# A hybrid attention and convolution layer: the norm of the second half of the sequence in steps of one engine's part, and the sums of w_down in fixed places of the convolution

## The chip, the cores and the metric

The kernel runs on one core of a Trainium2 chip. The metric is the device time of one execution in microseconds; the time before is the median of three runs. The engines are named as the profile names them: PE (matrix products) and PEld (its weight loads), DVE (vector), ACT (scalar, activations), POOL, and SP, which issues nearly all DMAs. Each engine works through its own instructions in order; semaphores tie the engines together.

## What is computed

The reference is one layer on a sequence of 2048 rows of width 1024, in float32:

```python
h = rmsnorm(x, norm1_g) * (1 + sc1) + sh1
proj = h @ w_in
q, k, v, fg, xin, bg, cg = jnp.split(proj, IN_SPLITS, axis=-1)
q = rmsnorm(q.reshape(b, s, ATTN_HEADS, HEAD_DIM), q_norm_g)
k = rmsnorm(k.reshape(b, s, ATTN_HEADS, HEAD_DIM), k_norm_g)
attn = forgetting_attention(q, k, v, logf).reshape(b, s, ATTN_WIDTH)
conv = bg * causal_dwconv(cg * xin, conv_mix_w)
x = x + g1 * (jnp.concatenate([attn, conv], axis=-1) @ w_out)
h2 = rmsnorm(x, norm2_g) * (1 + sc2) + sh2
u_gate, u_val = jnp.split(causal_dwconv(h2 @ w_up, ffn_conv_w), 2, axis=-1)
y = (jax.nn.silu(u_gate) * u_val) @ w_down
return x + g2 * y
```

The shifts, scales and gates (`sh1`, `sc1`, `g1`, ...) come from a small product of the condition `c`. The attention has 8 heads of 64, the convolution 512 channels with 3 taps, the feed-forward part a hidden width of 2816.

## The kernel before

**Products.** Large products run as high and low parts: an operand is split into `hi`, its rounding to a shorter format, and `lo`, what is left, and three matmuls (hi·hi, hi·lo, lo·hi) are added up. The two products of the feed-forward part also use a scheme of seven block products in place of eight, with sums and differences of blocks as operands. For `w_down`, four of these block sums per unit of 256 rows are worked out once, early in the kernel, and kept in DRAM as `w_sc`; there are 11 units (`NJ`).

**Stages.** By the trace: start, modulation and the value product to about 180 us; the k and q projections (`project`, L605 to L665) to 360; the convolution (`for j in range(4)`, L815 to L890) to 605; attention to about 935; the output product and the first residual to 1130; then, for each half of the sequence, `up` (the product with `w_up`, the 3-tap convolution and the gate) and `down` (the product with `w_down` and the last residual): `up(0)` to 1530, `down(0)` to 1777, `up(1)` to 2175, `down(1)` to 2388.

**What sets the order.** An instruction wrapped in `K` (`tc.keep_in_program_order`, L141) keeps its place among the others that are wrapped; those that are not wrapped are placed by a scheduler, in time and so on their engine. Work that runs beside the matmuls is written as Python generators, of which the main loop takes a step at fixed places. Tiles come from pools by tag; a tag with `bufs=n` has n buffers, and a new tile waits until the one before it in that buffer is done with.

**The sums of w_down.** `down_sums` (L742 to L768) loads two tiles `wd` for each unit, one unit ahead, makes four sums of 128x512 into one tile `ws` of 128x2048 (`bufs=1`), and stores it with one DMA of 1 MB. None of this is wrapped. The convolution takes one of its steps with each of its three block products (`next(wsums)`, L851), 48 in all; the first load and the three steps of each unit use 34.

**The convolution.** For each of four channel groups and four chunks of the sequence it makes the products `x`, `c` and `b` in three of six PSUM banks, 24 matmuls with three parts each; ACT and DVE then combine them (L860 to L882).

**down(0).** Its loop goes over 77 entries `e`: 7 block products `p`, each over 11 units `j`. An entry is 12 matmuls (L1643), on four accumulators; the entry of `j` = 9 is done together with `j` = 10. Each entry needs an operand pair, `raw`, read from DRAM five entries ahead and split by ACT into `hi` (L1412) and by DVE into `lo` (L1413), two entries ahead; `raw`, `hi` and `lo` have four buffers each. At `j` = 10 of a product DVE or ACT takes the four sums out of PSUM (`evict`); for p = 1, 4, 5 and 6 this makes finished blocks of the output (`finish_block`), multiplied by the gate, added to `xs` (rows of x1, read again) and stored.

**The norm of the second half.** `x1`, the sequence after the first residual, is kept in DRAM as `x1_sc`. `norm2(Q)` makes the operands of `up` for quarter `Q` of the sequence. Quarters 0 and 1 are done before `up(0)`; 2 and 3 run beside `down(0)`, as its `side` generator, which takes a step in 45 of the 77 entries (L1646). For these quarters a step loads four tiles of 128x1024 (`w<-x_sc`, L1272); then come the sums of squares on ACT (L1276), two per step, the reciprocal root on DVE, the scaling on DVE (L1283), and for each of 8 columns of 128 a transposition on PE into `pt` (L1259), the affine part on ACT (L1261), and the parts `hi` (ACT, L1242) and `lo` (DVE, L1245). For quarter 3 each k of 4 takes two columns and makes from them and the columns of quarter 2 five operands, by the sums and differences of L1252 and L1317; a step holds operations of DVE and ACT that depend on one another.

Of the kernel before, what the change touches and what calls it, by code (L numbers as in the profile page):

```python
# [20 lines left out]
P = 128  # L21
# [25 lines left out]
def kernel(  # L47
# [104 lines left out]
    with ExitStack() as ph:  # L152
# [588 lines left out]
        def down_sums():  # L741

            todo = []

            def load(j):
                ab = [lp.tile([P, D], F32, tag="wd", name="wd", bufs=4) for _ in range(2)]
                for e, w in enumerate(ab):
                    nc.sync.dma_start(w, w_down[(2 * j + e) * P : (2 * j + e + 1) * P, :])
                todo.append(ab)

            load(0)
            yield
            for j in range(NJ):
                if j + 1 < NJ:
                    load(j + 1)
                (a11, a21), (a12, a22) = [[w[:, 0:512], w[:, 512:1024]] for w in todo.pop(0)]
                t = lp.tile([P, 2 * D], F32, tag="ws", name="ws", bufs=1)
                s1, s2, s3, s4 = [t[:, n * 512 : (n + 1) * 512] for n in range(4)]
                V.tensor_tensor(s1, a21, a22, op=ALU.add)
                yield  # L760
                V.tensor_tensor(s3, a11, a21, op=ALU.subtract)
# [5 lines left out]
            while True:  # L767
                yield  # L768

        wsums = down_sums()  # L770
# [450 lines left out]
    with ExitStack() as ph:  # L1221
# [10 lines left out]
        def add_gated(acc, gate, src, dst):  # L1232

            g = temp()
            K(V.tensor_tensor(g, acc, gate, op=ALU.mult))
            K(V.tensor_tensor(src, src, g, op=ALU.add))
            nc.sync.dma_start(dst, src)

        bt = {}

        def high(raw, hi):
# [2 lines left out]
        def low(raw, hi, lo):  # L1244
            K(V.tensor_tensor(lo, raw, hi, op=ALU.subtract))  # L1245
# [18 lines left out]
        def norm2(Q):  # L1264
# [4 lines left out]
            xn[Q] = kept[Q] if Q < 2 else [wide_temp()[:, 0:D] for _ in range(4)]  # L1269
            if Q >= 2:  # L1270
                for t in range(4):
                    K(nc.sync.dma_start(xn[Q][t], x1_sc[Q * 4 + t]))  # L1272
                yield
            for t in range(4):
                junk = fp.tile([P, D], BF16, tag="t2", name="junk", bufs=NTEMP)
                K(A.activation(junk, xn[Q][t], AF.Square, accum_out=ss[:, t : t + 1]))  # L1276
# [42 lines left out]
                yield  # L1319
            if Q % 2:  # L1320
                low(t4, *t4s)
                yield

        add = lambda o, a, b: K(V.tensor_tensor(o, a, b, op=ALU.add))  # L1324
# [249 lines left out]
        def down(hv, side):  # L1574
# [13 lines left out]
            def banks(kinds):  # L1588
# [2 lines left out]
                    for k in kinds  # L1591
                ]

            def finish_block(c, n, t, total):
                g = temp()
                K(V.tensor_tensor(g, total, gate[n], op=ALU.mult))
                add(xs[c, n][t], xs[c, n][t], g)
                K(nc.sync.dma_start(out[rows[c][t], n * 512 : (n + 1) * 512], xs[c, n][t]))

            def evict(p, t):  # L1600
                a = acc[t]
                if p == 0:
                    K(A.activation(u2[t], a, AF.Copy))
                elif p == 1:
                    finish_block(0, 0, t, a)
                elif p == 2:
                    add(u2[t], u2[t], a)
                elif p == 3:
                    add(u3[t], u2[t], a)
                elif p == 5:  # L1610
                    add(u3[t], u3[t], a)
                    finish_block(1, 1, t, u3[t])
                else:
                    g = temp()
                    add(g, u2[t], a)
                    finish_block(*((0, 1) if p == 4 else (1, 0)), t, g)

            extra = {(1, 2): (0, 0), (4, 2): (0, 1), (5, 2): (1, 1), (6, 3): (1, 0)}
            for e, (p, j) in enumerate(todo):
# [15 lines left out]
                if j != NJ - 2:  # L1635
                    for t in range(4):
# [6 lines left out]
                                K(T.matmul(acc[t], lhsT=a[:, c], rhs=b, start=st, stop=sp, skip_group_check=True))  # L1643
# [45 lines left out]
```

## Time and profile before

| | |
|---|---|
| median of 3 runs | 2398.73 us (2393.88 to 2399.53) |
| the profiled execution | 2397.5 us, its span 2395.8 us |
| granted clock of PE, mean | 0.992 |
| PE, DVE, ACT busy | 95%, 73%, 48% of the span |
| `down(0)` | 1529.8 to 1776.9: 247.1 us, clock 0.96 |
| `down(1)` | 2175.5 to 2388.3: 212.8 us, clock 1.00 |

Three views are used below. The windows give for a stretch the busy time of each engine, with the count of its instructions in parentheses, and the clock that PE was granted (1.00 is full speed). The timeline gives one row for an instruction or a run of like ones: start, duration, engine, line, operation, result `<-` operands, partitions x elements, count, and in brackets how long the engine had been idle and what ended that. The waits add these idle times up by the line that waited and what it waited for. DMA rows give size and the median time from issue to landing.

### The profile page before, as it was taken

How to read it: one execution, taken by the hardware profiler on the slowest of the kernel's cores; microseconds unless marked ns; L12 is line 12 of the kernel's file. 1: busy time of each engine (PE TensorE's matmuls, PEld its weight loads, DVE VectorE, ACT ScalarE, POOL GpSimd, SP SyncE). 2: the span in 40 equal slices, each digit the busy share in tenths (PEclk: the TensorE clock that was granted, in tenths of full speed). 3: DMA queues.
4: the chain of work that ended last, by engine and by line, in shares of the span. 5: the costliest groups of instructions: out<-in, count | busy, mean ns of one | idle time of the engine just before them, and what ended most of it. 6: DMA issues, size and time to landing. Idle time of an engine off the chain costs nothing.

```text
span 2395.8 us, 38576 instructions
## 1 busy us (share of the span) xinstructions
PE 2284.4 (95%) x14208; PEld 1359.9 (57%) x14208; DVE 1738.1 (73%) x3404; ACT 1161.1 (48%) x1990; POOL 340.0 (14%) x282
## 2 busy tenths in 40 slices
PE   5899999999899898999999999999899999999998
PEld 5764444444577676444444444577764444447886
DVE  6768896653899897456999999766755555656556
ACT  5745353321688897343556556454423223224332
POOL 0211111111677784001000000000000000000000
PEclk9999999999999999999999999999999999999999
DMA  9349898632799997434565565765664544455765
GB/s 278 138 156 270 274 265 280 204 106 88 147 182 182 209 188 150 169 110 167 174 212 198 204 221 195 254 221 193 211 205 143 161 156 145 154 162 188 236 198 209
DMA packets 447895, 455.25 MB, mean 190 GB/s; under 512 B 190721, under 2 KB 300633, under 8 KB 445273
## 3 DMA queue, kind: packets, MB, share of 16 engines
q1 hardware_dynamic: 440584, 435.94, 61.7%
q10 hardware_dynamic: 4752, 8.46, 1.0%
q0 software_dynamic: 2368, 8.39, 0.9%
q8 instruction: 111, 1.82, 0.3%
q14 instruction: 80, 0.65, 0.1%
HBM read 284.84 MB, written 134.28 MB: 175 GB/s over the span
## 4 chain that ended last, share of the span: by engine, by line
PE 72%; DVE 14%; DMA 5%; ACT 4%; issue 3%; SPq 1%; POOL 0%; DVEq 0%; ACTq 0%; POOLq 0%
PE acc L1489 28%; PE acc L1643 14%; PE pr L145 10%; PE acc L145 8%; PE pv L145 2%; PE pt L1099 2%; PE ps L1038 1%; PE ps L1039 1%; DVE near L1106 1%; DMA far<-wide 1%; DVE t L1324 1%; PE po L1135 1%; DVE s_t L1062 1%; DVE lo L1413 1%; PE po L1137 1%
## 5 line engine op out<-in xcount | busy, mean ns | idle before, releaser
L1489 PEld LDWEIGHTS <-pair 128*128 128x128 f16 x3696 | 361.5, 98 | 439.7 <-issue 5.0
L1489 PE MATMUL acc<-t,pair 128*128 128x512 f16 x2112 | 477.4, 379 | 1.9 <-DVE t L1324 1.9
L1489 PE MATMUL acc<-b,pair 128*128 128x512 f16 x1584 | 363.4, 379 | 0.0
L1502 DVE SCALAR_TENSOR_TENSOR w<-w,fcw,w 128x1024 f32<-128x1024 f32 x176 | 226.1, 1285 | 79.4 <-ACT w L1497 73.4
L1413 DVE TENSOR_TENSOR lo<-raw,hi 128x1024 fp32r<-128x1024 f32 x154 | 185.2, 1223 | 128.4 <-ACT hi L1412 114.6
L1643 PE MATMUL acc<-hi 128*128 128x512 f32 x616 | 245.5, 399 | 15.0 <-ACT hi L1412 10.2
L1643 PE MATMUL acc<-lo,hi 128*128 128x512 f32 x616 | 243.9, 396 | 4.7 <-DVE lo L1413 4.7
L1643 PE MATMUL acc<-hi,lo 128*128 128x512 f32 x616 | 242.9, 394 | 0.0
L1412 ACT ACTIVATE hi<-raw 128x1024 fp32r<-128x1024 f32 x154 | 158.8, 1053 | 165.3 <-PE acc L1643 96.6
L145 PEld LDWEIGHTS <-h 128*128 128x128 f16 x1344 | 130.7, 98 | 98.7 <-DVE h L358 5.4
L1497 ACT ACTIVATE w<-w,fcw 128x1024 f32<-128x1024 f32 x88 | 100.6, 1143 | 160.9 <-DVE w L1324 160.9
L145 PE MATMUL acc<-wp,mp 128*128 128x512 f16 x768 | 171.1, 382 | 1.1 <-DVE raw L991 1.0
L1079 ACT ACTIVATE s_t<-s_t,nb,cst 128x2048 f32<-128x2048 f32 (+15 forms) x128 | 164.7, 1288 | 4.8
L1643 PEld LDWEIGHTS acc<-hi 128*128 128x128 f32 x616 | 117.5, 191 | 43.6 <-ACT hi L1412 12.3
L1091 POOL TENSOR_TENSOR wide<-s_t,wide 128x1024 f16<-128x1024 f32 x64 | 136.7, 2136 | 5.3
L1643 PEld LDWEIGHTS acc<-lo,hi 128*128 128x128 f32 x616 | 117.4, 191 | 31.4 <-DVE lo L1413 7.7
L1062 DVE CUSTOM_DVE_ANT_0 s_t<-ps,nf,mx 128x512 f32<-128x512 f32 (+1 forms) x192 | 119.5, 643 | 17.0 <-PE ps L1041 8.9
L1643 PEld LDWEIGHTS acc<-hi,lo 128*128 128x128 f32 x616 | 117.4, 191 | 24.8
L145 PE MATMUL pr<-h,wh 128*128 128x512 f16 x576 | 126.5, 379 | 0.0
L145 PE MATMUL pr<-h,wl 128*128 128x512 f16 x576 | 125.8, 379 | 0.0
L145 PEld LDWEIGHTS <-mp 128*128 128x128 f16 x768 | 75.4, 98 | 88.9 <-issue 3.4
L1038 PE MATMUL ps<-kh,qs 128*128 128x512 f16 (+1 forms) x320 | 109.6, 347 | 5.3 <-DVE mx L1062 4.4
(355 smaller groups left out, 4085.4 us busy)
## 6 DMA issues: line engine op xcount, KB each, us to landing
up_sc<-pair SPq DMA_DIRECT2D x132, 256.0 KB, 2.7
pair<-up_sc SPq DMA_DIRECT2D x132, 256.0 KB, 3.2
wx<-in_w_up_dram SPq DMA_DIRECT2D x88, 256.0 KB, 3.8
raw<-in_w_up_dram SPq DMA_DIRECT2D x44, 512.0 KB, 3.8
y_t<-t SPq DMA_DIRECT2D x88, 256.0 KB, 2.7
raw<-y_t SPq DMA_DIRECT2D x88, 256.0 KB, 4.1
raw<-w_sc SPq DMA_DIRECT2D x88, 256.0 KB, 4.2
y_b<-y SPq DMA_DIRECT2D x66, 256.0 KB, 2.1
```

The costliest lines, as they stand in the source:

```text
L145: ins = T.matmul(acc, lhsT=a, rhs=b, start=st, stop=sp)
L1038: K(T.matmul(ps[:, 0:cw], lhsT=qt, rhs=kh[:, c0 : c0 + cw], start=True, stop=False))
L1062: K(V.tensor_tensor_reduce(out=s_t[:, o0 + c0 : o0 + c0 + cw], in0=ps[:, 0:cw], in1=nf[:, c0 : c0 + cw], scale=1.0, scalar=-3.0e38 if g == ...
L1079: K(A.activation(cols, cols, AF.Exp, bias=nb[:, p : p + 1], scale=qk[:, 4:5], accum_out=un["l"][:, p : p + 1]))
L1091: K(G.tensor_tensor(wide[:, 1, :], s_t[:, WB * P : WU], wide[:, 0, :], op=ALU.subtract))
L1099: K(T.transpose(pt[:, b * P : (b + 1) * P], s_t[:, (b0 + b) * P : (b0 + b + 1) * P], ident))
L1412: K(A.activation(hi, raw, AF.Copy))
L1413: K(V.tensor_tensor(lo, raw, hi.bitcast(F32), op=ALU.subtract))
L1489: K(T.matmul(acc, lhsT=a, rhs=b, start=st, stop=sp, skip_group_check=True))
L1497: K(A.activation(y, u[:, 0:1024], AF.Copy, scale=fcw[:, ct : ct + 1]))
L1502: K(V.scalar_tensor_tensor(y, u[:, m : m + 1024], fcw[:, m * 44 + ct : m * 44 + ct + 1], y, op0=ALU.mult, op1=ALU.add))
L1643: K(T.matmul(acc[t], lhsT=a[:, c], rhs=b, start=st, stop=sp, skip_group_check=True))
```

## The change

It has two parts that don't touch each other.

The sums of `w_down`: loads, sums and stores are now wrapped in `K`, so they stand where the convolution takes a step. Each sum has a tile of its own (128x512, six buffers) and a DMA of its own (256 KB; 44 in place of 11), which is issued at the first step of the next unit.

The norm of quarters 2 and 3: `norm2_late` takes the place of `norm2`, and `down` takes a step of it in every entry. The load is issued in the first step of a quarter, two further steps do nothing, then comes one square per step. A column's transposition, its affine part with `hi`, and its `lo` stand in different steps. For quarter 3 the sums of a k (`sums`) are seven steps, of which each holds one engine's operations; they run while the next k's columns are transposed. Sixty-five entries have such work, in place of 39 steps before. `finish_block` and `evict` take their temporary `g` from the tag `first` with two buffers, no longer from `temp()` with seven.

```diff
@@ down_sums
-                    nc.sync.dma_start(w, w_down[(2 * j + e) * P : (2 * j + e + 1) * P, :])
+                    K(nc.sync.dma_start(w, w_down[(2 * j + e) * P : (2 * j + e + 1) * P, :]))
...
+            def keep(j, n, src0, src1, op):
+                t = lp.tile([P, 512], F32, tag="ws", name="ws", bufs=6)
+                K(V.tensor_tensor(t, src0, src1, op=op))
+                kept.append(lambda: K(nc.sync.dma_start(w_sc[j][:, n * 512 : (n + 1) * 512], t)))
+                return t
...
+                while kept:
+                    kept.pop(0)()
...
-                t = lp.tile([P, 2 * D], F32, tag="ws", name="ws", bufs=1)
...
-                V.tensor_tensor(s1, a21, a22, op=ALU.add)
-                yield
-                V.tensor_tensor(s3, a11, a21, op=ALU.subtract)
-                V.tensor_tensor(s2, s1, a11, op=ALU.subtract)
-                yield
-                V.tensor_tensor(s4, a12, s2, op=ALU.subtract)
-                nc.sync.dma_start(w_sc[j], t)
+                s1 = keep(j, 0, a21, a22, ALU.add)
+                yield
+                keep(j, 2, a11, a21, ALU.subtract)
+                s2 = keep(j, 1, s1, a11, ALU.subtract)
+                yield
+                keep(j, 3, a12, s2, ALU.subtract)
                 yield
@@ norm2_late (new, for Q = 2 and 3)
+            for t in range(4):
+                K(nc.sync.dma_start(xn[Q][t], x1_sc[Q * 4 + t]))
+            for _ in range(3):
+                yield
+            for t in range(4):
+                junk = fp.tile([P, D], BF16, tag="t2", name="junk", bufs=NTEMP)
+                K(A.activation(junk, xn[Q][t], AF.Square, accum_out=ss[:, t : t + 1]))
+                yield
...
+            def sums(k, b1, b2):
...
+                high(b2, b22[0])
+                diff(t3, b2, b1)
+                diff(b1, b1, b11[0])
+                diff(b1, b1, b11[1])
+                low(b2, *b22)
+                yield
+                high(b1, t1s[0])
+                high(t3, t3s[0])
+                yield
+                diff(b2, b2, b1)
+                low(b1, *t1s)
+                low(t3, *t3s)
+                yield
+                high(b2, t2s[0])
+                yield
...
+            for k in range(4):
+                first = turn(Q, k)
+                go_on()
+                yield
+                b1 = first()
+                go_on()
+                yield
+                second = turn(Q, 4 + k)
+                go_on()
+                yield
+                b2 = second()
+                go_on()
+                running.append(sums(k, b1, b2))
+                yield
@@ down
+            def rest():
+                return fp.tile([P, 1024], F32, tag="first", name="g", bufs=2)[:, 0:512]
...
-                g = temp()
+                g = rest()
...
-                if e < 3 or e % 2 == 0 or e % 7 == 1:
-                    next(side, None)
+                next(side, None)
...
-        steps = {Q: norm2(Q) for Q in range(4)}
+        steps = {Q: (norm2 if Q < 2 else norm2_late)(Q) for Q in range(4)}
```

How the rows move on the engines, at three places. First ACT in `down(0)`, where quarter 2 arrives; `hi` are the splits of `down`'s operands, `junk` the squares of the four loaded tiles. Before:

```order
L1412 ACTIVATE hi<-raw 128x1024 x5
L1276 ACTIVATE junk,ss<-w_18779 128x1024
L1276 ACTIVATE junk,ss<-w_18780 128x1024
L1412 ACTIVATE hi<-raw 128x1024 x2
L1276 ACTIVATE junk,ss<-w_18781 128x1024
L1276 ACTIVATE junk,ss<-w_18782 128x1024
L1412 ACTIVATE hi<-raw 128x1024 x2
```

And now:

```order
L1514 ACTIVATE hi<-raw 128x1024 x5
L1344 ACTIVATE junk,ss<-w_18823 128x1024
L1514 ACTIVATE hi<-raw 128x1024
L1344 ACTIVATE junk,ss<-w_18824 128x1024
L1514 ACTIVATE hi<-raw 128x1024
L1344 ACTIVATE junk,ss<-w_18825 128x1024
L1514 ACTIVATE hi<-raw 128x1024
L1344 ACTIVATE junk,ss<-w_18826 128x1024
L1514 ACTIVATE hi<-raw 128x1024
```

The squares, two and two before, now stand one by one between the splits.

Second, DVE at the end of product 4 of `down(0)`: three rows (`u,acc`, then the gate, then `xs`) are the eviction of the last of four sums, and the rows below it belong to the sums of quarter 3 (`t_...`) and to the operands of the next entries (`lo`). Before:

```order
L1324 TENSOR_TENSOR t_20051<-u,acc 128x512
L1596 TENSOR_TENSOR t_20053<-t_20051,gates 128x512
L1324 TENSOR_TENSOR xs<-xs,t_20053 128x512
L1252 TENSOR_TENSOR t_19936<-t_19936,b_19166 128x512
L1252 TENSOR_TENSOR t_19982<-t_19982,t_19936 128x512
L1245 TENSOR_TENSOR t_19987<-t_19936,t_19987 128x512
L1245 TENSOR_TENSOR t_19989<-t_19984,t_19989 128x512
L1413 TENSOR_TENSOR lo<-raw,hi 128x1024 x2
L1252 TENSOR_TENSOR t_19985<-b_19246,t_19982 128x512
```

And now:

```order
L1426 TENSOR_TENSOR g<-u,acc 128x512
L1701 TENSOR_TENSOR g<-g,gates 128x512
L1426 TENSOR_TENSOR xs<-xs,g 128x512
L1246 TENSOR_TENSOR t_19944<-t_20049,t_19944 128x512
L1253 TENSOR_TENSOR t_20022<-t_20022,t_19970 128x512
L1246 TENSOR_TENSOR t_20054<-t_19970,t_20054 128x512
L1246 TENSOR_TENSOR t_20056<-t_20058,t_20056 128x512
L1515 TENSOR_TENSOR lo<-raw,hi 128x1024 x2
L1253 TENSOR_TENSOR t_20185<-b_19350,t_20022 128x512
```

Four operations of the sums, three `lo` and one difference, stand between the eviction and `lo`; before there were two differences and two `lo`.

ACT at the same place, where `pt` is the transposed column and L1242 (now L1243) makes the `hi` of the sums. Before:

```order
L1261 ACTIVATE t_19982<-pt,sh_225,a_224 128x512
L1242 ACTIVATE b_19986<-t_19982 128x512
L1412 ACTIVATE hi<-raw 128x1024 x2
L1242 ACTIVATE t_19987<-t_19936 128x512
L1242 ACTIVATE t_19989<-t_19984 128x512
L1242 ACTIVATE t_19988<-t_19982 128x512
L1412 ACTIVATE hi<-raw 128x1024 x2
```

And now:

```order
L1243 ACTIVATE b_20053<-t_20022 128x512
L1514 ACTIVATE hi<-raw 128x1024
L1329 ACTIVATE t_20071<-pt,sh_225,a_224 128x512
L1243 ACTIVATE t_19944<-t_20049 128x512
L1243 ACTIVATE t_20054<-t_19970 128x512
L1243 ACTIVATE t_20056<-t_20058 128x512
L1514 ACTIVATE hi<-raw 128x1024 x2
```

Before, the operands of the three `hi` of the sums (`t_19936`, `t_19984`, `t_19982`) include the two that DVE changes behind the eviction (rows L1252 above). Now `t_20049`, `t_19970` and `t_20058` are ready before DVE's eviction; the difference behind it writes `t_20022`, which ACT reads in a later step.

Third, DVE in the k projection; `ws` are sums of `w_down`, L132 and L655 the norm of k. Before:

```order
L132 SCALAR_TENSOR_TENSOR r<-rqt,rqy 128x8
L759 TENSOR_TENSOR ws<-wd 128x512
L655 TENSOR_TENSOR qn<-acc,r 128x512
L762 TENSOR_TENSOR ws<-ws,wd 128x512
L764 TENSOR_TENSOR ws<-wd,ws 128x512
```

And now:

```order
L132 SCALAR_TENSOR_TENSOR r<-rqt,rqy 128x8
L655 TENSOR_TENSOR qn<-acc,r 128x512
L651 TENSOR_REDUCE r<-sq 128x8
L175 TENSOR_REDUCE group<-pt 1x1
L652 TENSOR_SCALAR r<-r,group 128x8
```

28 of the 44 sums stood among the rows of the projections before, and none does now. They stand in the convolution, where L866 and L879 combine its products:

```order
L753 TENSOR_TENSOR ws<-wd 128x512
L631 TENSOR_TENSOR tl<-tf,th 128x512
L601 SCALAR_TENSOR_TENSOR vo<-vt,vs,vo 128x8x64
L753 TENSOR_TENSOR ws<-wd 128x512
L753 TENSOR_TENSOR ws<-ws,wd 128x512
L879 SCALAR_TENSOR_TENSOR y<-z,cst,y 128x512
L880 SCALAR_TENSOR_TENSOR y<-z,cst,y 128x512
L881 TENSOR_TENSOR y<-y,bt 128x512
```

The first sums of a unit are now at these places, in the order in which the convolution takes its steps. PE's rows differ in `down(0)` alone, POOL's nowhere.

More of the change, by code (lines that the diff above doesn't have):

```diff
@@ L747, in load @@
                 for e, w in enumerate(ab):
-                    nc.sync.dma_start(w, w_down[(2 * j + e) * P : (2 * j + e + 1) * P, :])
+                    K(nc.sync.dma_start(w, w_down[(2 * j + e) * P : (2 * j + e + 1) * P, :]))
                 todo.append(ab)
+            def keep(j, n, src0, src1, op):
[3 more added lines that the diff above has]
+                return t
+            kept = []
             load(0)
@@ L755, in down_sums @@
                     load(j + 1)
+                while kept:
+                    kept.pop(0)()
                 (a11, a21), (a12, a22) = [[w[:, 0:512], w[:, 512:1024]] for w in todo.pop(0)]
-                t = lp.tile([P, 2 * D], F32, tag="ws", name="ws", bufs=1)
-                s1, s2, s3, s4 = [t[:, n * 512 : (n + 1) * 512] for n in range(4)]
-                V.tensor_tensor(s1, a21, a22, op=ALU.add)
+                s1 = keep(j, 0, a21, a22, ALU.add)
                 yield
-                V.tensor_tensor(s3, a11, a21, op=ALU.subtract)
-                V.tensor_tensor(s2, s1, a11, op=ALU.subtract)
+                keep(j, 2, a11, a21, ALU.subtract)
+                s2 = keep(j, 1, s1, a11, ALU.subtract)
                 yield
-                V.tensor_tensor(s4, a12, s2, op=ALU.subtract)
-                nc.sync.dma_start(w_sc[j], t)
+                keep(j, 3, a12, s2, ALU.subtract)
                 yield
             while True:
+                while kept:
+                    kept.pop(0)()
                 yield
@@ L1230, in wide_temp @@
             return fp.tile([P, 1040], F32, tag="w4", name="w4", bufs=5)[:, 0:1026]
-        def add_gated(acc, gate, src, dst):
-            g = temp()
-            K(V.tensor_tensor(g, acc, gate, op=ALU.mult))
-            K(V.tensor_tensor(src, src, g, op=ALU.add))
-            nc.sync.dma_start(dst, src)
         bt = {}
@@ L1268, in norm2 @@
             ss = fp.tile([P, 16], F32, tag="ss", name="ss", bufs=2)[:, 0:4]
[L1269 to L1272, printed above, removed]
-                yield
+            xn[Q] = kept[Q]
             for t in range(4):
@@ L1613, in evict @@
                 else:
-                    g = temp()
+                    g = rest()
                     add(g, u2[t], a)
```

55 lines of the change are left out of this document (54 added, 1 removed).

## The prediction

> **What bounds the kernel now.** I began with the head of the page, then took the stretches in which the two halves of the second matrix product (`down`, first half `down(0)`, second half `down(1)`) and the earlier stages ran, one row for each stretch.
>
> ```profile
> span 2395.8 us, 38576 instructions
> PE 2284.4 (95%) x14208; PEld 1359.9 (57%) x14208; DVE 1738.1 (73%) x3404; ACT 1161.1 (48%) x1990; POOL 340.0 (14%) x282
> ```
>
> TensorE (PE) is busy for 95% of the span, so a change can gain only where PE waits or runs at a lower clock: 111 us in all. The windows below have, after the length, the busy time of PE, PEld, DVE, ACT and POOL, and then PE's granted clock.
>
> ```profile
> 1529.80:1776.90 247.10, 229.45 (x991) 184.22 (x990) 168.13 (x215) 114.38 (x141) 0.00 (x0) 0.96 0.65 217
> 2175.50:2388.30 212.80, 210.72 (x926) 173.15 (x924) 127.81 (x129) 81.50 (x80) 0.00 (x0) 1.00 0.67 217
> 240.00:300.00 60.00, 57.08 (x284) 28.20 (x283) 53.41 (x185) 21.80 (x47) 6.17 (x9) 1.00 0.90 275
> 420.00:480.00 60.00, 60.00 (x285) 28.19 (x284) 39.76 (x90) 23.32 (x57) 6.75 (x8) 1.00 0.64 204
> ```
>
> The first two rows are `down(0)` and `down(1)`: the same matmuls, 34.3 us apart, and only the first carries the norm of the second half beside it. The third row is a stretch of the projections, where PE loses 2.9 us; the fourth is in the convolution, where PE loses nothing and DVE is busy for 40 of 60 us. These are the places that the change touches. Next, PE's waits within `down(0)`, and the rows of the timeline at which they lie (start, duration, operation, in brackets the wait and who ended it).
>
> ```profile
> PE acc L1643 <- ACT hi L1412: 10.2, 4, 5.7
> PE acc L1643 <- DVE lo L1413: 4.1, 6, 0.8
> PE acc L1643 <- DVE u L1324: 3.3, 3, 1.2
> ```
>
> ```profile
> 1535.23 0.39 PE L1643 MATMUL acc<-hi,lo 128*128 128x512 f32 x1
> 1535.46 0.39 PE L1643 MATMUL acc<-hi 128*128 128x512 f32 x1
> ...
> 1555.19 0.50 PE L1643 MATMUL acc<-hi 128*128 128x512 f32 x1 [0.53 <-ACT hi L1412]
> ...
> 1558.84 0.50 PE L1643 MATMUL acc<-hi 128*128 128x512 f32 x1 [1.66 <-ACT hi L1412]
> ...
> 1627.77 0.50 PE L1643 MATMUL acc<-hi 128*128 128x512 f32 x1 [2.31 <-ACT hi L1412]
> ...
> 1630.05 0.63 PE L1643 MATMUL acc<-hi 128*128 128x512 f32 x1
> 1630.47 0.63 PE L1643 MATMUL acc<-lo,hi 128*128 128x512 f32 x1
> ...
> 1635.08 0.39 PE L1643 MATMUL acc<-hi 128*128 128x512 f32 x1
> ...
> 1713.24 0.79 PE L1643 MATMUL acc<-hi 128*128 128x512 f32 x1 [5.71 <-ACT hi L1412]
> ...
> 1747.19 0.50 PE L1643 MATMUL acc<-hi 128*128 128x512 f32 x1 [1.09 <-DVE u L1324]
> ```
>
> Waits add up to 17.6 us. The rest is clock: a matmul starts 0.23 us behind the one before it (1535.23 to 1535.46), but 0.42 us behind it after a wait (1630.05 to 1630.47), until 1635.08. An entry of `down` (12 matmuls) is thus 12 × 0.227 = 2.72 us.
>
> **What of it can be had.** The first half also transposes the normalised rows on PE, which `down(1)` does not.
>
> ```profile
> 1577.15 0.60 PE L1259 MATMUL pt<-ident,w 128*128 128x128 f32 x4
> 1577.51 0.48 PE L1643 MATMUL acc<-hi 128*128 128x512 f32 x1
> ```
>
> Four transposes hold the next matmul back by 0.36 us, and I add 0.08 for the slower start of that matmul: 0.44. Sixteen such groups make 7.0 us. So `down(0)` without any harm from the side work would take 212.8 + 7.0 = 219.8 us, and at most 247.1 − 219.8 = 27.3 us can be recovered there.
>
> **The change part by part: the squares behind the load.** These are ACT and SP (the DMA issues) where the rows of the second half arrive.
>
> ```profile
> 1545.82 2.79 SPq L1272 DMA_DIRECT2D w<-x_sc  x4
> ```
>
> ```profile
> 1551.48 1.06 ACT L1276 ACTIVATE junk<-w 128x1024 bf16<-128x1024 f32 x1 [5.64 <-DMA w<-x_sc]
> ...
> 1557.73 1.06 ACT L1412 ACTIVATE hi<-raw 128x1024 fp32r<-128x1024 f32 x1 [2.60 <-DMA raw<-in_w_down_dram]
> ...
> 1710.57 1.67 ACT L1242 ACTIVATE t<-t 128x512 f16<-128x512 f32 x3 [10.60 <-DVE t L1252]
> 1712.15 1.99 ACT L1412 ACTIVATE hi<-raw 128x1024 fp32r<-128x1024 f32 x2
> ```
>
> ACT stands 5.64 us at the first square until the load lands (issued 1545.82, square at 1551.48: 5.7 us), and `hi` of `down`'s operands is queued behind it; PE then runs dry at 1555.19 and 1558.84. The same happens for the fourth quarter at 1627.77. What each costs with its clock: from 1554.27, the last matmul at full pace, to 1563.25 twelve steps of 0.227 are 2.7 us, and 9.0 passed: 6.3 us. For the other, from the wait's start near 1625.1 to 1635.08, fifteen steps are 3.4 us, and 10.0 passed: 6.6 us. Together 12.9 us. After the change the squares stand three entries behind the load, 3 × 2.72 = 8.2 us against 5.7 us to landing, so ACT meets data that is there, with 2.5 us to spare. One square and one `hi` per entry are 1.06 + 1.06 = 2.1 us of ACT against 2.72 us of PE, so ACT keeps up. I take the whole 12.9 us as gained. The bound from below is 6.6, where the quarter-three stall (in which the row at 1557.73 waits for a load of `raw`, not for the rows) stays: a rival below. What comes late next is DVE.
>
> **The column sums beside the eviction of p = 4.** The largest wait, 5.71 us at 1713.24, is a chain through both engines: DVE evicts four sums of product 4, then makes the difference that ACT's three `t` wait for (10.60 us), and `hi` stands behind those.
>
> ```profile
> 1701.65 0.68 DVE L1324 TENSOR_TENSOR t<-u,acc 128x512 f32<-128x512 f32 x1
> ...
> 1709.24 0.69 DVE L1324 TENSOR_TENSOR xs<-xs,t 128x512 f32<-128x512 f32 x1
> 1709.85 0.68 DVE L1252 TENSOR_TENSOR t<-t,b 128x512 f32<-128x512 f32 x1
> ...
> 1713.22 2.36 DVE L1413 TENSOR_TENSOR lo<-raw,hi 128x1024 fp32r<-128x1024 f32 x2 [0.69 <-ACT hi L1412]
> ```
>
> Twelve operations from 1701.65 to 1709.93: 0.69 each, 8.3 us. PE ran dry at 1713.24 − 5.71 = 1707.5, so the eviction ended 2.4 us too late, and the difference, three `t` and one `hi` were the rest. In the new order one step is one engine's part, and ACT's `t` there need nothing of the eviction, so `hi` is ready early. But DVE still has the eviction, then four operations of the sums (4 × 0.69 = 2.8), and then `lo` (2.36 / 2 = 1.2): 2.4 + 2.8 + 1.2 = 6.4 us behind PE's dry point, if the eviction starts where it does now. If DVE were free the moment PE stops a sum, it would end three operations behind the last sum, two entries less 2.1 us, so 3.4 us, before PE is dry, and the 4.0 us of the rest would leave a wait of 0.6. So the stall lies between 0.6 and 6.4 us. I take 5, near the upper end, because DVE is full there: one k of the sums is 11 operations of 0.69 and four `lo` of 1.2, 12.3 us, against four entries and two groups of transposes on PE, 11.8 us. It will be a wait for `lo` on DVE. The slow clock behind it costs half of a stretch of 3.4 us (the two slow stretches above end at 1563.25 and 1635.08, 21 times 3.42 us apart) or of two: 1.7 to 3.4 us, taken as 2.4.
>
> The smaller waits (1747.19 and its like, 4.5 us with their clock, and some 2 us elsewhere) fall together with evictions; the norm is drained by entry 64 in the new order, so there they should shrink to what `down(1)` has, which the floor holds already. That `g` comes from a pool of two buffers instead of seven costs nothing: each is read by the next DVE operation but one, and DVE runs in order.
>
> Sum for `down(0)`: 219.8 + 5 + 2.4 = 227.2 us, a gain of 19.9 us, between 13 and 25.
>
> **The sums of w_down.** In the projections the sums waited for their loads or for the store of the single tile, with DVE's other work behind them.
>
> ```profile
> 190.29 0.69 DVE L761 TENSOR_TENSOR ws<-wd 128x512 f32<-128x512 f32 x1 [3.27 <-DMA wd<-in_w_down_dram]
> 279.03 0.68 DVE L759 TENSOR_TENSOR ws<-wd 128x512 f32<-128x512 f32 x1
> ```
>
> ```profile
> 200.53 0.63 ACT L732 ACTIVATE wx<-wx 128x512 f32<-128x512 f32 x1 [3.85 <-DMA wx<-in_w_up_dram]
> 281.03 0.72 ACT L600 ACTIVATE vo<-vt,vs 128x512 f16<-128x512 f32 x1 [4.29 <-DMA vt<-v_sc]
> ```
>
> ```profile
> 202.37 0.27 PE L579 MATMUL pt<-ident,vm 128*1 128x128 f32 x1 [1.20 <-ACT tf L629]
> 284.44 0.66 PE L623 MATMUL pt<-ident,qn 128*128 128x128 f32 x4 [2.20 <-ACT tf L629]
> ```
>
> The two PE waits, 1.20 and 2.20 us, lie about 12 and 5 us behind such sums, through a store that SP issued late, a load behind it on SP and an ACT operation behind that. With 28 sums and 14 loads gone from the projections I take both as gained, 3.4 us; the bounds are 0 (other loads are as late: DMA is 0.90 busy there) and 6 us.
>
> In the convolution the 28 sums add 28 × 0.69 = 19 us to DVE, over 240 us of which it uses two thirds (39.76 of 60), and 33 more stores go through SP. What covers both: PE holds a finished chunk of three sums in three of six banks while it fills the other three, 15.6 us ahead. The row that shows how far that reaches is SP standing still for 8 us there while PE stays at 60.00 of 60:
>
> ```profile
> 382.39 8.04 SPq L748 DMA_DIRECT2D wd<-in_w_down_dram  x3
> ```
>
> So I cost it at nothing. The cost if the cover went is a rival.
>
> **Rivals.** *DVE has no lead at all.* Where every microsecond of DVE's surplus in entries 44 to 59 reaches PE, the stall is not 5 but 4 × 0.5 + 8.3 = 10.3 us, in several pieces, with about 4 us of slow clock: 219.8 + 14.3 = 234.1, a gain of 13 + 3.4, 2381 us. For it speaks that DVE's 12.3 exceed PE's 11.8; against, that operands are split up to three entries (8.2 us) ahead. The Trainium skill, "TensorE: Matmul & The Clock Gate", Part 1, has the clock fall only after an idle window of about 3.4 us; by that these pieces would cost no clock and this rival would end at 2377, but the trace goes slow from 1630.05 to 1635 behind waits of 2.31 and at most 0.8 us, so the trace disagrees and 2381 stands.
>
> *The raw operands are late, not the rows.* The 2.60 us wait at 1557.73 was for `raw`. If the four loads of rows ahead in the queues make it late, 6.3 us stay: 2380 us. Against it: `raw` has four buffers, which came free late because ACT stood.
>
> *Slower: the convolution waits.* Pinned sums put DVE's evictions behind loads and SP behind 44 stores. A unit spans three of PE's sums of 5.2 us, 15.6 us; it decides whether the steps of a unit, if each held up the next, take longer than that. They would: SP's 8.0, the load's 5.8 and the store's 2.7 below, four sums of 0.69, 19.3 us, 3.7 too many, and 11 × 3.7 = 41 us on top of 2375 give 2416. Against it: loads run a unit ahead and stores a step behind, so they overlap, the 8.04 us cost nothing at 382, and DVE has a third of its time free. The size of the stores bears on this:
>
> ```profile
> y_t<-t SPq DMA_DIRECT2D x88, 256.0 KB, 2.7
> ```
>
> ```profile
> wd<-in_w_down_dram SPq DMA_DIRECT2D x22, 512.0 KB, 5.8
> w_sc<-ws SPq DMA_DIRECT2D x11, 1024.0 KB, 6.4
> ```
>
> Four of 2.7 us are 10.8 against 6.4 for one of 1 MB, if they ran one after another; six tiles and the next step's delay hide that. The Trainium skill, "DMA: Bandwidth & Descriptors", Bandwidth, advises at least 1 MiB for each DMA to reach 75% of the peak, which speaks against the split; the two rows agree, and by it the 11 units would hold the queues for 48 us longer, which is a cost only where something waits.
>
> *Nothing moves.* The places that PE waits for shift, and the next late thing takes the same time: 2396 us. For it speaks only the fullness of DVE.
>
> **The numbers.** Forecast 2397.5 − 19.9 − 3.4 = 2374.2 for an execution like the profiled one; this lies 1.2 us under the median of the runs shown, so 2375. Chances: forecast 0.60, no lead 0.17, raw late 0.13, nothing 0.06, slower 0.04. The range takes in the bounds: best 27 + 6 gives 2366, and both smaller rivals together about 2388; 2365 to 2388. A measurement here tells 0.3%, 7.2 us: faster 0.90, same 0.06, slower 0.04.
>
> **What would show it.** Right: `down(0)` near 227 us in its window; no wait of ACT for the rows of x1; PE's largest wait near entry 57, for `lo` of DVE; PE at 60.00 of 60 in the convolution; no `ws` before it. Wrong: waits for `hi` remaining around 1555 or 1627 (raw late), waits of a microsecond or two spread over entries 44 to 59 (no lead), PE under 60 of 60 between 360 and 600 (the slower rival).

## The result, and the profile after

The changed kernel takes 2373.73 us (median of 4 runs, 2372.73 to 2379.02), the kernel before 2396.65 us beside it (4 runs, 2393.88 to 2399.53): a ratio of 0.9909, 95% interval 0.9888 to 0.9929, 22.9 us. The forecast was 2375. The total is right; its two terms are not, as the stages show.

The prediction counts the quarters of the sequence from one: its quarters three and four are Q = 2 and Q = 3 of the code, which the diffs and the expectations call quarters 2 and 3. Below they are Q = 2 and Q = 3. A slow matmul is one that starts 0.42 us behind the one before it, in place of 0.23.

First the windows of the changed kernel's profiled execution (2379.0 us, span 2377.3): `down(0)`, the projections, and a piece of the convolution; then the projections before. The last two numbers of a row are the busy share of the DMA engines and the GB/s that they moved.

```profile
1521.54:1755.11 233.57, 223.74 (x990) 182.35 (x989) 167.40 (x215) 116.26 (x141) 0.00 (x0) 0.98 0.70 230
180.00:360.00 180.00, 179.48 (x904) 90.79 (x903) 152.98 (x558) 90.79 (x204) 21.17 (x34) 1.00 0.73 201
420.00:480.00 60.00, 60.00 (x283) 27.91 (x281) 44.13 (x95) 19.62 (x46) 6.94 (x8) 1.00 0.92 292
```

```profile
180.00:360.00 180.00, 173.46 (x860) 86.34 (x859) 162.84 (x582) 87.99 (x199) 19.62 (x30) 0.99 0.91 269
```

`down(0)` went from 247.1 to 233.6 us, not to 227.2: 13.5 us. It begins 8.3 us earlier (1521.5 against 1529.8), and the projections show why: PE is busy for 179.5 of 180 us there, before 173.5. In the convolution PE is busy all the time, as before. The two stages give 21.8 us. The rest of the span moves by some microseconds from one execution to the next: of the kernels below, those with the new sums and no extra additions begin `down(0)` between 1517.4 and 1520.7, and the one with the old sums at 1534.0. In this execution `down(1)` took 3 us more, which the last section comes back to.

PE's waits in `down(0)`, and the rows of the timeline at which they lie:

```profile
PE acc L1748 <- DVE lo L1515: 6.6, 3, 5.1
PE acc L1748 <- ACT hi L1514: 1.9, 2, 1.6
PE acc L1748 <- DVE u L1426: 1.4, 2, 1.1
```

```profile
1546.62 0.49 PE L1748 MATMUL acc<-hi 128*128 128x512 f32 x1 [0.24 <-ACT hi L1514]
...
1550.23 0.51 PE L1748 MATMUL acc<-hi 128*128 128x512 f32 x1 [1.61 <-ACT hi L1514]
...
1696.25 0.80 PE L1748 MATMUL acc<-lo,hi 128*128 128x512 f32 x1 [5.06 <-DVE lo L1515]
1696.84 0.63 PE L1748 MATMUL acc<-hi,lo 128*128 128x512 f32 x1
```

17.6 us of waits became 9.9. Nothing waits at the arrival of Q = 3 any more (1627.77 before). At that of Q = 2 the waits stand where they stood, at 25 and 29 us into the stage. The big wait of entry 57 is 5.06 us, of a matmul that reads `lo`, where it was 5.71 for `hi`; slow matmuls follow it.

Why the first group stayed is seen on ACT and SP:

```profile
1538.13 1.06 ACT L1344 ACTIVATE junk<-w 128x1024 bf16<-128x1024 f32 x1 [0.47 <-DMA w<-x_sc]
...
1545.51 1.06 ACT L1514 ACTIVATE hi<-raw 128x1024 fp32r<-128x1024 f32 x1 [6.24 <-DMA raw<-in_w_down_dram]
```

```profile
1533.69 1.93 SPq L1339 DMA_DIRECT2D w<-x_sc  x4
1535.72 0.50 SPq L1525 DMA_DIRECT2D raw<-y_b  x1
1536.26 0.47 SPq L1532 DMA_DIRECT2D raw<-in_w_down_dram  x1
```

ACT waits 0.47 us for the rows, not 5.64: that part of the change does what it says, though with less margin than forecast, since ACT came to the square 4.0 us after the loads were issued (1533.69) and not three entries, 8.2 us, after. But then `hi` waits 6.24 us for its own operand. By order of issue that is the `raw` sent at 1535.72 to 1536.26, right behind the four loads of rows, and it took about 9 us to land. Behind the loads of Q = 3 `hi` waits for a `raw` too, 1.18 us at 1624.32, but that wait did not reach PE.

The wait of entry 57, on DVE:

```profile
1684.37 0.68 DVE L1426 TENSOR_TENSOR g<-u,acc 128x512 f32<-128x512 f32 x1
...
1692.57 0.68 DVE L1246 TENSOR_TENSOR t<-t,t 128x512 f16<-128x512 f32 x1
...
1694.97 2.35 DVE L1515 TENSOR_TENSOR lo<-raw,hi 128x1024 fp32r<-128x1024 f32 x2
```

Twelve operations of the eviction, four of the sums, then `lo`, without a gap: the order that the forecast walked through by hand.

### The profile page after: what moved, and what is told of

Read it like the earlier page. It is cut to its first block, busy times and chain, and to the rows that moved or that the text cites. A ratio compares the mean times of both kernels' runs of the same rounds, so it can differ in the third digit from the quotient of the medians.

```text
span 2377.3 us, 38568 instructions
## 1 busy us (share of the span) xinstructions
PE 2277.8 (96%) x14208; PEld 1359.0 (57%) x14208; DVE 1740.6 (73%) x3404; ACT 1163.9 (49%) x1990; POOL 339.0 (14%) x282
## 4 chain that ended last, share of the span: by engine, by line
PE 78%; DVE 11%; DMA 4%; ACT 4%; issue 2%; SPq 1%; POOL 0%; DVEq 0%; ACTq 0%
PE acc L1591 28%; PE acc L1748 14%; PE acc L145 13%; PE pr L145 10%; PE pv L145 2%; PE pt L1107 2%; PE ps L1046 1%; DMA far<-wide 1%; PE ps L1047 1%; DVE near L1114 1%; PE po L1143 1%; DVE s_t L1070 1%; ACT s_t L1087 1%; PE po L1145 1%; PE po L1144 1%
```

## The experiments

The kernel before took 2397.8, 2398.5 and 2400.0 us beside the three groups of runs; ratios are to the one beside them, with a 95% interval in brackets, and are not quotients of the two medians.

**The changed kernel again**

> The changed kernel itself, to stand beside the other three on the same chip: 2373.7 us within 4 us.

2374.02 us (2373.20 to 2376.44), ratio 0.9901 (0.9884 to 0.9918).

**One part alone.** The first kernel keeps the old `down_sums`. The second is the kernel before with the new sums alone; two places in which it differs from the changed kernel are shown:

```diff
-        steps = {Q: (norm2 if Q < 2 else norm2_late)(Q) for Q in range(4)}
+        steps = {Q: norm2(Q) for Q in range(4)}
...
-                next(side, None)
+                if e < 3 or e % 2 == 0 or e % 7 == 1:
+                    next(side, None)
```

> The new norm with the old sums of w_down. Theory (two separate gains): only down(0) gets shorter, to about 233.6 us as in the changed kernel, while the stretch 180 to 360 keeps its 6.5 us of PE waits; the whole is 13 to 14 us faster than before, about 2383 us. Rival (the parts need each other): the whole gain is here or none of it, 2374 or 2396 us.

> The new sums of w_down with the old norm. Theory: PE's waits between 180 and 360 fall from 6.5 us to under 1 us and the convolution keeps PE at full; down(0) stays at 247 us; the whole is about 8 us faster than before, about 2388.5 us. Rival (what the forecast held): 3.4 us faster, 2393 us. Slower rival: PE waits in the convolution, 2400 us or more.

The norm alone: 2385.87 us, ratio 0.9939 (0.9922 to 0.9955). The sums alone: 2387.08 us, 0.9948 (0.9933 to 0.9963). The windows, `down(0)` and the projections of each, first of the norm alone, then of the sums alone:

```profile
1534.00:1767.60 233.60, 223.95 (x990) 182.38 (x988) 167.35 (x215) 116.36 (x141) 0.00 (x0) 0.98 0.70 230
180.00:360.00 180.00, 173.12 (x844) 86.20 (x843) 160.38 (x571) 88.07 (x201) 19.64 (x30) 0.97 0.89 265
```

```profile
1517.84:1766.09 248.25, 229.93 (x990) 183.66 (x989) 168.08 (x215) 114.50 (x141) 0.00 (x0) 0.96 0.66 216
180.00:360.00 180.00, 179.48 (x904) 90.75 (x903) 152.34 (x556) 90.63 (x205) 21.32 (x34) 1.00 0.73 202
```

Each part acts in its own stage alone: 12.0 and 10.7 us by the medians, which add up to 22.7 of the 22.9. By the intervals the first is 11 to 19 us and the second 9 to 16, so the close agreement is in part chance. The sums are worth about three times the 3.4 us of the forecast.

**Why the sums were dear in the projections.** One kernel puts the traffic back without the additions, one puts additions back without the traffic.

```diff
+                if col == AW and i % 2 and i > 2:
+                    for e, sw in enumerate(spare.pop(0)):
+                        K(nc.sync.dma_start(w_sc[i // 2 - 1][:, e * D : (e + 1) * D], sw))
+                if col == AW and i % 2 == 0 and i < 14:
+                    spare.append([lp.tile([P, D], F32, tag="wd", name="wd", bufs=4) for _ in range(2)])
+                    for e, sw in enumerate(spare[-1]):
+                        K(nc.sync.dma_start(sw, w_down[(i + e) * P : (i + e + 1) * P, :]))
```

> The changed kernel, with the DMA traffic of seven units (14 loads of 512 KB, 14 stores of 512 KB, of no use) put into the k projection, and no sums on DVE there. Theory (DVE's work stood behind sums that waited for data): PE's waits between 180 and 360 us stay under 1 us, time as the changed kernel, 2374 us. Rival (the traffic itself makes other loads late): PE waits 3 us or more there again, about 2380 us.

```diff
+                if col == AW and i < 14:
+                    for _ in range(2):
+                        t5 = lp.tile([P, 512], F32, tag="ws", name="ws", bufs=6)
+                        K(V.tensor_tensor(t5.rearrange("p (h d) -> p h d", d=DH), qn, qn, op=ALU.add))
```

> The changed kernel, with 28 more additions of 128x512 on DVE in the k projection (of no use, on data that is there), and no more DMA. If DVE's time there were the cause of the old waits, PE waits 2 us or more between 180 and 360 us; if it was that the sums waited for data, PE waits under 1 us and the time is that of the changed kernel, 2374 us.

With the traffic: 2372.43 us, ratio 0.9884 (0.9864 to 0.9904). With the additions: 2379.85 us, 0.9915 (0.9893 to 0.9937). The windows from 180 to 360 us, of the traffic and of the additions, and then the first matmul of attention, of the kernel before, the changed one, the one with the traffic and the one with the additions:

```profile
180.00:360.00 180.00, 179.36 (x904) 90.66 (x903) 153.65 (x562) 91.01 (x204) 21.16 (x34) 1.00 0.93 279
```

```profile
180.00:360.00 180.00, 176.88 (x886) 88.49 (x885) 167.11 (x591) 89.99 (x204) 19.27 (x32) 1.00 0.69 194
```

```profile
605.91 0.38 PE L1038 MATMUL ps<-kh,qs 128*128 128x512 f16 x1 [0.73 <-DVE cst L793]
595.70 0.38 PE L1046 MATMUL ps<-kh,qs 128*128 128x512 f16 x1 [0.73 <-DVE cst L801]
596.38 0.38 PE L1055 MATMUL ps<-kh,qs 128*128 128x512 f16 x1 [0.73 <-DVE cst L810]
600.71 0.38 PE L1050 MATMUL ps<-kh,qs 128*128 128x512 f16 x1 [0.73 <-DVE cst L805]
```

The traffic costs nothing even at 0.93 DMA busy. The additions alone, on data that is there, cost PE 2.6 us in this window, where the old sums cost 6.0. Up to the start of attention they cost 5.0 us of 10.2, known within some 2 us, since the other kernels with the new sums come there between 595.2 and 597.7; over the whole kernel some 6 us, by two runs alone. So the idea that only the waiting sums did it is wrong: PE waits over 2 us there, the sign that was named for DVE's time as the cause. But the additions explain only about half of the old loss. That the other half is the sums' waiting for data is what is left when both are taken away; it was not shown by itself.

**One store of 1 MB, in the convolution.** The sums wrapped in `K`, but with the old tile (`bufs=1`) and the old store.

```diff
-                s1 = keep(j, 0, a21, a22, ALU.add)
+                K(V.tensor_tensor(s1, a21, a22, op=ALU.add))
...
+                K(nc.sync.dma_start(w_sc[j], t))
```

> The changed kernel, with the sums in fixed places of the convolution, but one tile of 128x2048 with one buffer and one store of 1 MB for each unit, as before. Theory (PE is a chunk ahead there and covers all of it): DVE waits for each store, PE does not wait in the convolution, and the time is that of the changed kernel, 2374 us within 3 us. Rival (the store of 1 MB holds DVE long enough for PE): PE under 60 of 60 us in the convolution, 2380 us or more. If small stores cost bandwidth, this one is faster than the changed kernel.

2375.33 us, ratio 0.9891 (0.9873 to 0.9909): no difference from the changed kernel. PE's window over the convolution, and DVE's wait there:

```profile
360.00:590.00 230.00, 230.00 (x1081) 107.44 (x1080) 142.75 (x283) 64.76 (x146) 31.18 (x30) 1.00 0.69 229
```

```profile
DVE ws L759 <- DMA w_sc<-ws: 8.3, 5, 3.7
```

DVE waits 8.3 us for the store, in five waits, and PE never. What matters is the place of the sums, not the six tiles or the 44 stores. In the changed kernel the small stores spare DVE nothing, and they land no faster than the large one did before (6.4 us):

```profile
DVE ws L753 <- DMA w_sc<-ws: 15.4, 7, 3.8
```

```profile
w_sc<-ws SPq DMA_DIRECT2D x44, 256.0 KB, 6.0
```

**Is `raw` late because of the loads of rows?** One kernel leaves these loads out (`G.memset(xn[Q][t], 1.0)` for Q = 2, so POOL writes ones); one spreads them over the three entries that had nothing to do.

```diff
             for t in range(4):
                 K(nc.sync.dma_start(xn[Q][t], x1_sc[Q * 4 + t]))
-            for _ in range(3):
-                yield
+                if Q == 2 and t < 3:
+                    yield
+            if Q != 2:
+                for _ in range(3):
+                    yield
```

> The changed kernel without the loads of quarter 2: POOL writes ones into these tiles, so the output of that quarter is not the reference's. Theory (raw waits behind these loads): the waits near entry 9 are under 0.5 us, down(0) about 227.5 us. Rival (raw is late for its own sake or for the stores of y): the waits stay at 2 us or more, down(0) 232 us or more.

> The changed kernel, with the four loads of quarter 2 in four entries (3 to 6) in place of all in entry 3; every other step stands where it stood. Theory (the raw operands wait behind the four loads): the waits near entry 9 (3.4 us, 6.2 us with the slow clock) shrink to under 2 us and down(0) to about 228 us; 4 to 5 us faster than the changed kernel. Rival (the DMA engines have too much to move in that stretch, in whatever order): the waits stay at 3 us or more, or move by an entry or two, down(0) 232 us or more.

Without the loads: 2368.31 us (one run), and these windows and waits:

```profile
1518.97:1746.14 227.17, 220.54 (x990) 180.93 (x989) 167.23 (x215) 116.17 (x141) 2.87 (x3) 0.98 0.70 227
```

```profile
PE acc L1751 <- DVE lo L1518: 5.1, 1, 5.1
PE acc L1751 <- DVE u L1429: 1.6, 2, 1.1
```

The whole group near entry 9 is gone, and `down(0)` takes 227.2 us, the forecast's number; that it fits to the tenth is chance. So `raw` is late because of these loads. Whether by SP's time to issue them or by what they move is not told apart. Spread: 2369.64 us, ratio 0.9878 (0.9864 to 0.9893), `down(0)` 229.0 us, PE's waits and the row of ACT that is left:

```profile
PE acc L1751 <- DVE lo L1518: 5.8, 2, 5.1
PE acc L1751 <- ACT hi L1517: 1.3, 1, 1.3
```

```profile
1544.36 1.06 ACT L1347 ACTIVATE junk<-w 128x1024 bf16<-128x1024 f32 x1 [4.20 <-DMA w<-x_sc]
```

Of 3.4 us of waits 2.1 stay (1.32 for `hi`, 0.76 for `lo`), just over the 2 us expected, and no slow clock behind them. Now a square waits 4.20 us for its own load again: the second load, issued at 1535.99, stands among those of `raw` and lands 8.4 us later, and three entries are too few for it. The times of theory and run agree within a microsecond.

**No norm beside the eviction**

```diff
-                next(side, None)
+                if hv or e not in (52, 53, 54, 55, 56):
+                    next(side, None)
```

> The changed kernel, with no step of the norm in entries 52 to 56 of down(0), so that nothing of it lies beside or behind the eviction of p = 4. Theory (eviction plus sums fill DVE): the wait of 5.06 us for lo shrinks to under 1 us, and down(0) from 233.6 to about 226 us, 7 to 8 us faster than the changed kernel. Rival (DVE has no lead in the whole stretch of the sums, or the sums meet the next eviction): waits of the same sum appear at entries 57 to 70, down(0) 231 us or more.

2374.75 us, ratio 0.9899 (0.9884 to 0.9913), `down(0)` 234.0 us: nothing gained. PE's waits:

```profile
PE acc L1748 <- DVE lo L1515: 3.5, 6, 0.8
PE acc L1748 <- DVE u L1426: 2.5, 3, 1.1
PE acc L1748 <- ACT hi L1514: 2.5, 3, 1.3
```

The wait of entry 57 is 0.68, but the sums, five entries later, now meet the eviction of p = 5, and eight waits of 0.26 to 1.08 us from 1689 on, with thirteen slow matmuls among them, add up to the same. Of the two rivals the one by which the sums meet the next eviction was right.

**Part of the eviction on POOL** (here and in the next kernel `rest` also hands out both halves of its two tiles, which is not shown)

```diff
-                g = rest()
-                K(V.tensor_tensor(g, total, gate[n], op=ALU.mult))
-                add(xs[c, n][t], xs[c, n][t], g)
+                E = G if (c, n) in ((0, 1), (1, 1)) else V
+                g = total if (c, n) == (0, 1) else rest()
+                K(E.tensor_tensor(g, total, gate[n], op=ALU.mult))
+                K(E.tensor_tensor(xs[c, n][t], xs[c, n][t], g, op=ALU.add))
```

> The changed kernel, with the product with the gate and the sum with x1 for the blocks of p = 4 and p = 5 in both halves on POOL, which has no work in down. Theory (DVE's time behind the eviction is the wait): DVE has 8 operations less at p = 4, 5.5 us, and the wait of 5.06 us falls to 0.6 us or less; down(0) about 226 us, and some 7 us less than the changed kernel, 2367 us. Rival (POOL and DVE get in each other's way, DVE's operations take longer by a third or more): the wait stays over 3 us, 2372 us or more.

2394.31 us, ratio 0.9979 (0.9969 to 0.9990): 20 us worse than the changed kernel. `down(0)` takes 241.4 us and `down(1)`, which has the same edit, 226.2 in place of 213. DVE, POOL and SP there:

```profile
1685.40 1.65 DVE L1246 TENSOR_TENSOR t<-t,t 128x512 f16<-128x512 f32 x1
...
1692.06 4.50 DVE L1515 TENSOR_TENSOR lo<-raw,hi 128x1024 fp32r<-128x1024 f32 x2
```

```profile
1685.21 1.30 POOL L1708 TENSOR_TENSOR xs<-xs,g 128x512 f32<-128x512 f32 x1
1686.46 1.74 POOL L1707 TENSOR_TENSOR g<-g,gates 128x512 f32<-128x512 f32 x1
```

```profile
1724.34 10.92 SPq L1709 DMA_DIRECT2D out_dram<-xs  x4
```

While POOL works, the same DVE operations take 1.65 in place of 0.68 us and `lo` 2.25 in place of 1.18: what DVE gave away it lost in pace, and PE's wait at entry 57 is still 4.56 us: the rival was right. At p = 5 SP, which stores the blocks, stands 10.9 us in its queue until POOL is done, and the loads of `raw` stand behind it; PE then waits 3.96 us at 1741.61. The same two waits are there in `down(1)`, 5.07 and 3.73 us. The second cost was in neither theory.

**Eight operations later, on DVE**

```diff
+                    if p == 4 and hv == 0:
+                        late.append(lambda: finish_block(0, 1, t, g))
+                    else:
+                        finish_block(*((0, 1) if p == 4 else (1, 0)), t, g)
...
                 next(side, None)
+                if late and e >= 60:
+                    late.pop(0)()
```

> The changed kernel, with eight of the twelve DVE operations of the eviction of p = 4 in down(0) (product with the gate, sum with x1) put off to entries 60 to 63; only the four that free PSUM stay. All stays on DVE. Theory (DVE's time ahead of lo at entry 57 is the wait): 8 x 0.61 = 4.9 us less ahead of lo, the wait of 5.06 us falls under 0.6 us and its slow clock goes; down(0) from 233.6 to about 226 us, 7 us less than the changed kernel. Rival (DVE is short over the whole stretch, as the entries 57 to 70 were when the norm was paused): waits of 3 us or more come back at entries 57 to 66, down(0) 231 us or more.

2370.14 us, ratio 0.9884 (0.9867 to 0.9901); its `down(0)` and waits:

```profile
1518.20:1747.79 229.59, 221.58 (x990) 180.28 (x989) 166.79 (x215) 116.36 (x141) 0.00 (x0) 0.99 0.71 234
```

```profile
PE acc L1756 <- DVE lo L1515: 3.6, 4, 1.6
PE acc L1756 <- DVE u L1426: 2.9, 3, 1.1
```

The wait of entry 57 is 0.54 us and its slow clock is gone, as the theory had it; but 1.56 us for `lo` come back 16 us later, where the eight operations stand now, and the eviction of p = 5 loses more (2.9 against 1.4 us). Four of seven microseconds are kept: both theories hold in part.

**Both**

> The changed kernel with both the loads of quarter 2 spread over four entries and the eight operations put off. Theory (the two waits are separate): down(0) about 221 to 222 us, near the 219.8 us of the floor, and about 11 us less than the changed kernel, 2362 us. Rival (one wait stands behind the other): no more than the better of the two alone, 2367 us.

2366.24 us (2362.47 to 2371.27), ratio 0.9866 (0.9847 to 0.9886): faster than the kernel before and than the changed one, 7.8 us below the latter beside it, with no overlap of the runs. `down(0)`:

```profile
1517.40:1746.07 228.67, 222.40 (x990) 180.98 (x988) 166.72 (x215) 116.58 (x141) 0.00 (x0) 0.99 0.71 235
```

That is 229 and not 221: twelve slow matmuls follow three waits of 0.74, 1.09 and 0.81 us at the eviction of p = 5 in this execution. The time is the rival's, 2367, and the runs overlap with those of either edit alone (2369.64 and 2370.14), so that both together gain more than one is not shown. Yet it is not that one wait stands behind the other: the `hi` wait near entry 9 (0.80) and that of entry 57 (0.53) are both short here. The gain is lost later, at the next eviction.

## Why the prediction was right in its sum and wrong in two of its terms

- **The loads of rows, Q = 3:** right. 6.6 us were to go and the group is not there after.
- **The loads of rows, Q = 2:** the step that failed is "I take the whole 12.9 us as gained". ACT's wait for the rows did end, with 0.47 us left. But the four loads stand ahead of `raw` in either order, and `raw` is late behind them whether ACT waits for the rows or not. The rival that gave 6.3 us for it, at 0.13, was the right one, and `no_load` shows the cause: without the loads the term comes out as forecast. The argument against that rival, that `raw`'s buffers came free late because ACT stood, was the wrong one; the wait of 2.60 us for `raw` at 1557.73, which the prediction shows, was already this one.
- **The eviction of p = 4:** right. 5 us for `lo` were forecast, 5.06 came. The clock behind it was 2.4 us; twelve slow matmuls are 12 × 0.20 = 2.4.
- **The rival in which DVE has no lead:** not in the changed kernel, which has one wait and not many. The paused and the deferred kernel show that it is near: when the work is moved by a few entries, the wait comes back in pieces.
- **The sums of w_down:** the step that failed is "I take both as gained, 3.4 us", with a bound of 6. The waits that had no sum beside them went as well, and the slow clock; the sums alone gave 10.7 us. I followed two waits back and left out that DVE, 163 of 180 us busy there, can be late for everything: additions without any wait cost some 5 of the 10 us up to attention. What made the other half is argued, not shown.
- **The convolution:** right. PE 60.00 of 60. The slower rival did not come, not even with one tile and the 1 MB store, so the price of 19.3 us per unit was never near: its parts overlap.
- **The size of the stores:** 2.7 us for 256 KB was taken from another store; here each took 6.0, and the large one 6.4, so the four must run beside one another. The advice of the Trainium skill, "DMA: Bandwidth & Descriptors", Bandwidth, to use at least 1 MiB per DMA, made no difference that can be measured here (2375.3 with it, 2373.7 and 2374.0 without), since PE waits for none of these stores, though DVE does.

So `down(0)` took 6.4 us more than forecast and the sums gave some 7 us more than forecast, and by luck the two errors met in a sum that was off by 1 us. The total says nothing for either term.

## What to carry to other kernels

A wait for a load can be met in two ways, by using it later or by loading less at once. The first was enough for Q = 3; for Q = 2 the stage's own operands, issued right behind the burst, were late as well, and only the second helped. So look at what is issued right behind a burst. Work of an engine that is nearly full can cost even where it waits for nothing itself: follow the engine's load over the stage, not just the waits that can be traced back. When the work of a full engine is moved, find the next place where it meets something; here three of seven microseconds were given back there.

## What the runs showed of the hardware

**DVE beside POOL.** DVE operations on two SBUF tiles took 2.4 times as long while POOL worked on SBUF tiles (0.68 to 1.65 us); the four that read a PSUM tile, three of them beside POOL, did not:

```profile
1683.01 2.48 DVE L1426 TENSOR_TENSOR g<-u,acc 128x512 f32<-128x512 f32 x4
```

The Trainium skill, "SBUF — State Buffer", "SBUF: two separate sides", says that DVE with two SBUF inputs and a GpSimd operation that reads SBUF hold a common pair of ports in turn, each for its whole instruction. The trace fits this: a POOL operation of 1.30 us, of which DVE waits for what is left, and DVE's own 0.6 make 1.9 at most, and DVE's rows are 1.65 to 1.78.

**Short waits and the clock.** The granted clock also fell without any wait as long as the slow stretch itself. In `down(1)`, where both kernels do the same, the profiled execution of the changed kernel has

```profile
2338.01 0.50 PE L1748 MATMUL acc<-hi 128*128 128x512 f32 x1 [1.08 <-DVE u L1426]
...
2340.06 0.76 PE L1748 MATMUL acc<-hi 128*128 128x512 f32 x1 [1.08 <-DVE u L1426]
2340.61 0.63 PE L1748 MATMUL acc<-lo,hi 128*128 128x512 f32 x1
```

and the second profiled execution of the same kernel (`after_again`)

```profile
2333.78 0.50 PE L1748 MATMUL acc<-hi 128*128 128x512 f32 x1 [0.61 <-DVE u L1426]
...
2335.83 0.50 PE L1748 MATMUL acc<-hi 128*128 128x512 f32 x1 [1.09 <-DVE u L1426]
```

with no slow matmul. Waits of 1.08 and 1.08 us within 3.2 us gave seven slow ones, 0.61 and 1.09 none; the first took 216.1 us for `down(1)`, the second 213.0. But the sum of the waits does not decide it. In `no_load`, at the same place,

```profile
2327.53 0.50 PE L1751 MATMUL acc<-hi 128*128 128x512 f32 x1 [0.50 <-DVE u L1429]
...
2329.58 0.50 PE L1751 MATMUL acc<-hi 128*128 128x512 f32 x1 [1.08 <-DVE u L1429]
```

are less than 0.61 and 1.09, and seven slow matmuls follow (from 2330.40). What decides it stays open. The Trainium skill, "TensorE: Matmul & The Clock Gate", Part 1, puts the slow clock after an idle window of about 3.4 us; the trace disagrees, since waits of 1.58 and of 2.16 us, both under two thirds of it, were enough here. Executions of one kernel differ by some 5 us, and this is one way in which they do.
